# Decode delta rule begun with its inputs, its state loads on ACT's queue, all gate units first, and shorter pauses in both delta-rule chains

## The chip, the cores and the metric

The kernel runs on 1 core of one Trainium2 chip. The metric is the device time of one launch in microseconds (us). The times of the kernel before are the median of 3 runs; one execution was also taken with the hardware profiler, and all rows below are from it.

## What is computed

One step of a decoder layer over 256 prompt tokens and 8 decode tokens (264 columns, `TT`), width 2048. The input is normalised and projected by one wide matrix into everything the layer needs. Branch (A) is a sparse attention; branch (B) is a gated delta rule. The lines that matter here:

```
xn = rms_norm(x, norm_w);  q, kv, ..., z_a, qkv_b, a, b, z_b, gate_a, gate_b = split_proj(xn @ w_in)
# (B), prompt: chunks of tokens, per head
A  = strict_lower(kb k^T * L);  Tm = inverse(eye + A)
u  = Tm @ vb;  w = Tm @ (kb * exp(dec));  vn = u - w @ S
o  = (q * exp(dec)) @ S + lower(q k^T * L) @ vn
S  = S * exp(dl) + (k * exp(dl - dec))^T @ vn
# (B), decode: the same rule with one token, for 8 sequences, each with its own state S (8 heads of 128 x 128)
y_a = (o_A * silu(z_a)) @ w_pa;  y_b = (rms_norm(o_B) * silu(z_b)) @ w_pb
y   = x + (sigmoid(gate_a) * y_a + sigmoid(gate_b) * y_b) @ w_o
```

The outputs are y for prompt and decode tokens, the new caches, and the new delta-rule states of the prompt (`o_S`) and of the 8 decode sequences (`o_Ss`, stored two sequences at a time).

## The kernel before

**The weight stream.** All big projections run as a list of weight halves (`halves`, class `W`): 512 KB of f32 weights (8 contraction tiles of 128 x 128) are loaded by SP into `raw`, split into a rounded high part `hi` by ACT (line 332) and a rest `lo` by DVE (line 333), and multiplied by PE in 24 matmuls of 264 columns (three products for each tile) into an accumulator bank `acc`, of which there are two. The main loop at the end of the program writes, for each half, the load of four halves on, the split of two halves on, its first 12 matmuls, a `tick()`, its other 12 matmuls (with the evacuation after a unit's last half), and another `tick()`. So there are two ticks to a half.

**The order of units.** `ORDER` (line 30) lists the units of the second part of the program, a letter each: k a column block of the delta rule's q, k, v; g and G a block of gate a and gate b (`ev_gate`, tanh by ACT); z and Z a block of the output gate of branch A and of branch B (`ev_z`: tanh into a tile `zt` at line 1460, two multiplications, the second by oA or oB at line 1462, and a split into `oh` and `ol`); p and P a block of the products with w_pa and w_pb, which read oh and ol as their operand (`ev_y`). A k, g, G, z or Z unit has two halves, a p or P unit one. The evacuation of the first Z unit (line 1456) calls `tick()` until the prompt rule has marked oB: whatever of the two chains is not written by then is written there, with no weights between.

**The chains.** Everything else is written by generators. A tick advances each active one once; `yield n` means that it goes on n ticks later. Two chains start after the last k unit: `g_gdn_dec` (line 1342), the decode rule, first in each tick, and `g_gdn`, the prompt rule. The decode rule makes its vectors (L1346 to 1394), pauses, and then takes the states in four blocks of two sequences: a load `sst` of 1 MB (line 1401), 32 small matmuls `sw`, two copies `swr` by ACT (line 1411), transposes `swt`, the new value `dvn` (line 1418), four times transposes `vnb` and an update of the state by ACT (line 1432) and DVE (line 1433), and the store `o_Ss` from ACT's queue (line 1436). The prompt rule makes its decay rows and the products `kk` for 8 heads (into `At` and `aT`), sends the diagonal blocks of At through DRAM (`ad`) into `lanes`, solves them there in 31 steps of a product into `prod` (line 1203) and a sum (line 1204), sends the result through DRAM (`td`, lines 1210 and 1211) into `U` and into `TI`, a part of prod, completes the inverse (`inv`), forms `uw`, and goes over two chunks (`vn`, `dS`, `og`; the state `Sg` is another part of prod), stores `o_S` (line 1318), normalises, waits for the decode rule's `odec`, and writes oB (`ogt`, line 1337).

**What sets the order.** SP and POOL run their instructions in the order in which the program writes them (`manual_schedule`). PE, ACT and DVE are ordered by the framework, which takes of the instructions that are ready the one written first. Tiles come from a few tags with a fixed number of buffers: `slot()` (line 169) gives 8 KB tiles of tag s8, 13 buffers (xt, qkvr, ktk, vbt, qT, At, aT, lanes, prod, U, wT, oG, oB, sst, gate, oh, ol and others); tag "a" has 5 buffers (zt, swr, P1, kbe, yt and others); each PSUM tag has 2. A buffer goes back when the last reader of its tile is done, a store among them.

Of the kernel before, what the change touches and what calls it, by code (L numbers as in the profile page):

```python
# [26 lines left out]
BIG = 1e30  # L27
NCMP = 127
PAST = 2048
ORDER = "kgkkgkgkkkkkgkkkkkgkkkkkkkkkkGzzggzzgggGGgzzzGzggppppppGpppggppppppgpZZZGZGGZZZZGGGGPPGPGGGPPPPPPPPPPPPP"  # L30


class Cols:
# [111 lines left out]
def program(tc, A):  # L145
    nc = tc.nc
    V, S, T, G, SP = nc.vector, nc.scalar, nc.tensor, nc.gpsimd, nc.sync
# [42 lines left out]
    def C(name, parts=128):  # L190
        o, n = C0[name]
        return cst[0:parts, o:o + n]
# [7 lines left out]
    def tr(out, in_):  # L200
        n = in_.shape[0]
        T.transpose(out, in_, ident[0:n, 0:n])  # L202
# [925 lines left out]
    def g_gdn():  # L1128
# [23 lines left out]
        for h in range(9):  # L1152
            if h < 8:
                pr = PG("rrow")
                for t in range(2):
                    tr(pr[:, 128 * t:128 * t + 128], dec[:, t, h:h + 1].to_broadcast([128, 128]))
                er = tp.tile([128, 256], F32, name="er", tag="a", bufs=NA)
                S.activation(er, pr[:, 0:256], AF.Exp)
                l1 = tp.tile([128, 2, 128], F32, name="l1", tag="a", bufs=NA)
                l2 = tp.tile([128, 2, 128], F32, name="l2", tag="a", bufs=NA)  # L1160
                for t in range(2):
                    V.scalar_tensor_tensor(l1[:, t], pr[:, 128 * t:128 * t + 128], dec[:, t, h:h + 1], C("mlow"),
                                           ALU.subtract, ALU.add)
                    V.scalar_tensor_tensor(l2[:, t], pr[:, 128 * t:128 * t + 128], dec[:, t, h:h + 1], C("mup"),
                                           ALU.subtract, ALU.add)
                S.activation(l1, l1, AF.Exp, scale=-1.0)
                S.activation(l2, l2, AF.Exp)
                V.tensor_copy(edl[:, h, :], er.rearrange("p (c i) -> p c i", c=2)[:, :, 127])
                lm[h] = l1, l2, er
            yield  # L1170
            if h:
                h1 = h - 1
                l1, l2, er = lm.pop(h1)
                pk = PG("kk")
                for t in range(2):
                    sl = slice(128 * t, 128 * t + 128)
                    mm(pk[:, 128 * t:128 * t + 128], kTg[:, h1, sl], kTg[:, h1, sl])
                    mm(pk[:, 256 + 128 * t:384 + 128 * t], kTg[:, h1, sl], qTg[:, h1, sl])
                for t in range(2):
                    V.scalar_tensor_tensor(At[:, t, h1, :], pk[:, 128 * t:128 * t + 128], be[:, t, h1:h1 + 1], l1[:, t],  # L1180
                                           ALU.mult, ALU.mult)
                V.tensor_mul(aT[:, :, h1, :], pk[:, 256:512].rearrange("p (t i) -> p t i", t=2), l2)
                V.tensor_tensor(qTg[:, h1, 0:TP], qTg[:, h1, 0:TP], er, ALU.mult)
            yield 4
        del L["qkv", 1], kTg

        ad = dp.tile([4, 16, 32, 32], F32, name="ad")
# [32 lines left out]
        for t in range(2):  # L1220
            for hg in range(2):
                p1 = PG("inv")
                for hh in range(4):
                    h = 4 * hg + hh
                    rhs = U[:, t, h, :].rearrange("p (c k j) -> p c k j", c=2, k=2)[:, :, 1, :]
                    mm(p1[:, 64 * hh:64 * hh + 64].rearrange("p (c j) -> p c j", c=2), At[:, t, h, :], rhs)
                yield 6
                P1 = tp.tile([128, 256], F32, name="P1", tag="a", bufs=NA)
                S.activation(P1, p1[:, 0:256], AF.Copy)
                yield  # L1230
                p2 = PG("inv")
                for hh in range(4):
                    for c in range(2):
                        pr = slice(64 * c, 64 * c + 32)
                        o = 64 * hh + 32 * c
                        mm(p2[pr, o:o + 32], TI[pr, 8 * t + 4 * hg + hh, :], P1[pr, o:o + 32])
                p2v = p2[:, 0:256].rearrange("p (h c j) -> p h c j", h=4, c=2)
                for c in range(2):
                    V.tensor_scalar(U[64 * c:64 * c + 32, t, 4 * hg:4 * hg + 4, 64 * c + 32:64 * c + 64],
                                    p2v[64 * c:64 * c + 32, :, c, :], -1.0, None, ALU.mult)  # L1240
# [22 lines left out]
        for h in range(8):  # L1263
            kb = tp.tile([128, 2, 128], F32, name="kbe", tag="a", bufs=NA)
            for t in range(2):
                V.tensor_scalar(kb[:, t], ktk[:, t, h, :], bed[:, t, h:h + 1], None, ALU.mult)
            for t in range(2):
                V.tensor_scalar(ktk[:, t, h, :], ktk[:, t, h, :], kds[:, t, h:h + 1], None, ALU.mult)
            yield
            pu = PG("uw")  # L1270
            for t in range(2):
                mm(pu[:, 128 * t:128 * t + 128], U[:, t, h, :], vbt[:, t, h, :])
                mm(pu[:, 256 + 128 * t:384 + 128 * t], kb[:, t], U[:, t, h, :])
            yield 3
            V.tensor_copy(uu[:, :, h, :], pu[:, 0:256].rearrange("p (t d) -> p t d", t=2))
            S.activation(wT[:, h, :], pu[:, 256:512], AF.Copy)
        del L["vbt"]
# [3 lines left out]
        for t in range(2):  # L1281
            tok = slice(128 * t, 128 * t + 128)
            if t:
                for hg in range(2):
                    hs = slice(4 * hg, 4 * hg + 4)
                    pv = PG("vn")
                    for hh in range(4):
                        h = 4 * hg + hh
                        mm(pv[:, 128 * hh:128 * hh + 128], wT[:, h, tok], Sg[:, h, :])
                    V.tensor_sub(uu[:, t, hs], uu[:, t, hs], pv.rearrange("p (h d) -> p h d", h=4))  # L1290
                yield 4
            vn = uu[:, t]
            for hg in range(2):
                hs = slice(4 * hg, 4 * hg + 4)
                pS = PG("dS")
                for hh in range(4):
                    h = 4 * hg + hh
                    mm(pS[:, 128 * hh:128 * hh + 128], ktk[:, t, h, :], vn[:, h, :])
                yield 4
                po = PG("og")  # L1300
                for hh in range(4):
                    h = 4 * hg + hh
                    if t:
                        mm(po[:, 128 * hh:128 * hh + 128], qTg[:, h, tok], Sg[:, h, :], start=True, stop=False)
                    mm(po[:, 128 * hh:128 * hh + 128], aT[:, t, h, :], vn[:, h, :], start=t == 0, stop=True)
                yield
                if t == 0:
                    V.tensor_copy(Sg[:, hs, :], pS.rearrange("p (h d) -> p h d", h=4))
                else:
                    for hh in range(4):  # L1310
                        h = 4 * hg + hh
                        V.scalar_tensor_tensor(Sg[:, h, :], Sg[:, h, :], edl[:, h, t:t + 1],
                                               pS[:, 128 * hh:128 * hh + 128], ALU.mult, ALU.add)
                for hh in range(4):
                    h = 4 * hg + hh
                    S.activation(oG[:, t, h], po[:, 128 * hh:128 * hh + 128], AF.Copy, scale=qss[:, t, h:h + 1])
                yield 4
        G.dma_start(A["o_S"], Sg)
        so = tp.tile([128, 2, 8], F32, name="so", tag="so")
        ro = tp.tile([128, 2, 8], F32, name="ro", tag="ro")  # L1320
# [21 lines left out]
    def g_gdn_dec():  # L1342
# [52 lines left out]
        od = tp.tile([128, 64], F32, name="dod", tag="dod")  # L1395
        vn = tp.tile([128, 64], F32, name="dvn", tag="dvn")
        hb3 = lambda a: a.rearrange("p (h b) -> p h b", h=8)
        yield 88
        for b0 in range(0, NB, 2):
            ss = slot("sst", [128, 2, 8, 128])  # L1400
            G.dma_start(ss, A["stS"][b0 // 2])
            yield
            yield 7
            p3 = PGD("sw")
            for b in range(2):
                for h in range(8):
# [11 lines left out]
            V.tensor_sub(a3(vn), a3(u), pv[:, 0])  # L1418
            V.tensor_mul(a3(od), a3(vn), a3(kq))
            V.tensor_add(a3(od), a3(od), pv[:, 1])  # L1420
            yield 7
            for b in range(2):
                for hg in range(2):
                    p4 = PGD("vnb")
                    for hh in range(4):
                        c = (4 * hg + hh) * 8 + b0 + b
                        tr(p4[:, 128 * hh:128 * hh + 128], vn[:, c:c + 1].to_broadcast([128, 128]))
                    yield 3
                    for hh in range(4):
                        h = 4 * hg + hh  # L1430
                        c = h * 8 + b0 + b
                        S.activation(ss[:, b, h, :], ss[:, b, h, :], AF.Copy, scale=eb[:, 0, c:c + 1])  # L1432
                        V.scalar_tensor_tensor(ss[:, b, h, :], p4[:, 128 * hh:128 * hh + 128], k[:, c:c + 1],
                                               ss[:, b, h, :], ALU.mult, ALU.add)
                    yield 10
            S.dma_start(A["o_Ss"][b0 // 2], ss)
        so = tp.tile([128, 64], F32, name="dso", tag="qrd")
        S.activation(so, od, AF.Square)
# [127 lines left out]
    for w, kind in ((0, "kvs"), (1, "kvw")):  # L1566
        for j in range(4):
            proj(kind, j, ev_kv(w, j))
            if w == 0 and j == 0:
# [4 lines left out]
              P=iter(range(16)))  # L1574
    for i, c in enumerate(ORDER):
        j = next(at[c])
# [136 lines left out]
```

## Time and profile before

| | us |
|---|---|
| median of 3 runs | 1161.1 |
| lowest, highest | 1159.9, 1166.39 |
| the profiled execution | 1159.74 |
| its span | 1158.1 |

PE is the engine that works nearly all the time; the page also gives each engine's busy time in 40 equal slices of the span, so that a slice is 28.95 us. Each digit is the busy share in tenths. The rows that are read for the change are in a section of their own below.

### The profile page before, as it was taken

The numbers are of one execution on the slowest core, as the hardware profiler recorded it, in microseconds if no ns is written. First come the engines' busy times: TensorE is split into PE (matmuls) and PEld (weight loads), VectorE is DVE, ScalarE is ACT, GpSimd is POOL, SyncE is SP. The second block draws the span as 40 slices with busy tenths as digits, with TensorE's granted clock in tenths as the row PEclk, the third lists the DMA queues.
The fourth block names the chain that finished last, engine by engine and source line by source line (L and its number), as shares of the span: only waits on it lengthen the run. The fifth ranks groups of instructions, "written<-read, shape, count | busy, mean of one in ns | idle before, by whom it ended". The sixth has DMA issues, their size and how long they took to land.

```text
span 1158.1 us, 24872 instructions
## 1 busy us (share of the span) xinstructions
PE 1113.8 (96%) x9334; PEld 1064.9 (92%) x9334; DVE 725.6 (63%) x1538; ACT 571.4 (49%) x1126; POOL 142.0 (12%) x221
## 2 busy tenths in 40 slices
PE   4999999999999999999999999999996799999998
PEld 4989999999999897987889999998995699999998
DVE  3587665443667776863565676899475555567543
ACT  4455655445544765763455444433445544344332
POOL 4420344100001410122113000000100000000000
PEclk9999999999999999999999999999998899999999
DMA  8875576335446974578979345555653255556663
GB/s 300 261 221 157 191 218 204 102 128 166 157 134 191 236 192 131 164 225 206 343 297 364 127 159 164 195 165 185 193 183 127 94 183 184 180 182 220 201 238 127
DMA packets 76843, 222.86 MB, mean 192 GB/s; under 512 B 10465, under 2 KB 27370, under 8 KB 75186
## 3 DMA queue, kind: packets, MB, share of 16 engines
q1 hardware_dynamic: 59346, 164.36, 43.3%
q0 software_dynamic: 15360, 49.90, 14.9%
q10 hardware_dynamic: 2016, 7.01, 1.6%
q8 instruction: 73, 1.20, 0.4%
q14 instruction: 48, 0.39, 0.1%
HBM read 203.23 MB, written 17.99 MB: 191 GB/s over the span
## 4 chain that ended last, share of the span: by engine, by line
PE 76%; issue 11%; DVE 4%; DMA 4%; SPq 2%; ACT 1%; POOL 1%; POOLq 1%; ACTq 0%; DVEq 0%
PE acc L205 64%; DVE lanes L1204 1%; PE po L205 1%; PE pvo L205 1%; DVE lo L333 1%; PE gtr L202 1%; DMA raw<-w 1%; PE ps L205 1%; PE gsc L205 1%; DMA rawc<-ccmp 1%; SPq L385 1%; SPq L386 1%; POOLq L385 1%; DMA o_wk<-wk 1%; ACT sst L1432 1%
## 5 line engine op out<-in xcount | busy, mean ns | idle before, releaser
L332 ACT ACTIVATE hi<-raw 128x1024 fp32r<-128x1024 f32 (+1 forms) x250 | 264.3, 1057 | 352.3 <-PE acc L205 300.7
L205 PE MATMUL acc<-xh,hi 128*128 128x264 f32 (+1 forms) x1488 | 434.0, 292 | 1.0 <-ACT hi L332 1.0
L205 PE MATMUL acc<-xl,hi 128*128 128x264 f32 (+1 forms) x1488 | 427.3, 287 | 0.0
L205 PE MATMUL acc<-xh,lo 128*128 128x264 f32 (+1 forms) x1488 | 426.0, 286 | 0.1
L333 DVE TENSOR_TENSOR lo<-raw,hi 128x1024 fp32r<-128x1024 f32 (+1 forms) x250 | 304.4, 1218 | 192.5 <-ACT hi L332 190.6
L205 PEld LDWEIGHTS acc<-xh,hi 128*128 128x128 f32 (+1 forms) x1488 | 281.2, 189 | 9.6 <-issue 8.9
L205 PEld LDWEIGHTS acc<-xl,hi 128*128 128x128 f32 (+1 forms) x1488 | 281.5, 189 | 1.2 <-issue 0.6
L205 PEld LDWEIGHTS acc<-xh,lo 128*128 128x128 f32 (+1 forms) x1488 | 280.3, 188 | 2.3 <-issue 1.4
L205 PE MATMUL acc<-hi,w1h 128*128 128x254 f32 (+1 forms) x512 | 147.4, 288 | 14.9 <-ACT hi L409 14.9
L205 PE MATMUL acc<-lo,w1h 128*128 128x254 f32 (+1 forms) x512 | 146.2, 286 | 4.1 <-DVE lo L410 3.8
L205 PE MATMUL acc<-hi,w1l 128*128 128x254 f32 (+1 forms) x512 | 144.7, 283 | 0.0
L410 DVE TENSOR_TENSOR lo<-rawc,hi 128x512 fp32r<-128x512 f32 (+2 forms) x136 | 84.1, 658 | 51.0 <-ACT hi L409 42.7
L205 PEld LDWEIGHTS acc<-hi,w1h 128*128 128x128 f32 x512 | 97.5, 191 | 15.3 <-ACT hi L409 15.1
L409 ACT ACTIVATE hi<-rawc 128x512 fp32r<-128x512 f32 (+2 forms) x136 | 74.5, 599 | 58.5 <-PE acc L205 54.3
L205 PEld LDWEIGHTS acc<-lo,w1h 128*128 128x128 f32 x512 | 98.1, 192 | 5.6 <-DVE lo L410 5.4
L205 PEld LDWEIGHTS acc<-hi,w1l 128*128 128x128 f32 x512 | 98.0, 191 | 0.1
L386 POOL DMA_DIRECT2D rawc<-ccmp x125 | 67.4, 539 | 98.1 <-issue 71.4
L205 PE MATMUL acc<-oh,hi 128*128 128x264 f32 x256 | 72.7, 284 | 1.6 <-DVE gate L1482 1.6
L205 PE MATMUL acc<-ol,hi 128*128 128x264 f32 x256 | 72.8, 285 | 0.0
L205 PE MATMUL acc<-mh,hi 128*128 128x264 f32 x256 | 72.6, 284 | 0.0
L205 PE MATMUL acc<-ml,hi 128*128 128x264 f32 x256 | 72.5, 283 | 0.0
L205 PE MATMUL acc<-oh,lo 128*128 128x264 f32 x256 | 72.5, 283 | 0.0
(451 smaller groups left out, 1495.0 us busy)
## 6 DMA issues: line engine op xcount, KB each, us to landing
raw<-win SPq DMA_DIRECT2D x184, 512.0 KB, 3.4
raw<-wpab SPq DMA_DIRECT2D x32, 512.0 KB, 3.5
raw<-wo SPq DMA_DIRECT2D x32, 512.0 KB, 3.8
rawc<-ccmp SPq DMA_DIRECT2D x126, 128.0 KB, 3.1
rawc<-ccmp POOLq DMA_DIRECT2D x125, 128.0 KB, 3.2
raw<-w SPq DMA_DIRECT2D x8, 512.0 KB, 4.4
wk<-winK SPq DMA_DIRECT2D x8, 512.0 KB, 7.1
o_wk<-wk POOLq DMA_DIRECT2D x8, 512.0 KB, 8.7
```

The source lines that it names most:

```text
L202: T.transpose(out, in_, ident[0:n, 0:n])
L205: T.matmul(out, lhsT, rhs, start=start, stop=stop, **k)
L332: S.activation(self.hi, self.raw, AF.Copy)
L333: V.tensor_sub(self.lo, self.raw, self.hi)
L385: r = e.value_load(ptf[0:1, b * NPG + j:b * NPG + j + 1], min_val=0, max_val=159)
L386: e.dma_start(rawc[kv, b][j // 8][:, j % 8].rearrange("p s c g -> p (s c g)"), src[kv, bass.ds(r, 1)].rearrange("o d f -> (o d) f"))
L409: S.activation(h, src, AF.Copy)
L410: V.tensor_sub(l, src, h)
L1204: V.tensor_reduce(Lt[:, i, 0:i], pp.rearrange("p j c -> p c j"), AX.X, ALU.add, negate=True)
L1432: S.activation(ss[:, b, h, :], ss[:, b, h, :], AF.Copy, scale=eb[:, 0, c:c + 1])
```

## The change

Four things: the string of units has all G ahead of all P; the pauses of the prompt rule are shortened (4 to 2, 6 to 3, 3 to 2, and others, as shown); the decode rule no longer pauses 88 ticks before its first state load, and its pauses between steps go from 7, 7, 3 and 10 to 4 (with one tick less beside it), 2, 2 and 2; and the state loads are issued by ACT instead of POOL.

```diff
@@ -27,7 +27,7 @@
 BIG = 1e30
 NCMP = 127
 PAST = 2048
-ORDER = "kgkkgkgkkkkkgkkkkkgkkkkkkkkkkGzzggzzgggGGgzzzGzggppppppGpppggppppppgpZZZGZGGZZZZGGGGPPGPGGGPPPPPPPPPPPPP"
+ORDER = "kgkkgkgkkkkkgkkkkkgkkkkkkkkkkGzzggzzgggGGgzzzGzggppppppGpppggppppppgpZZZGZGGZZZZGGGGGGGGPPPPPPPPPPPPPPPP"
 
 
 class Cols:
@@ -1181,7 +1181,7 @@
                                            ALU.mult, ALU.mult)
                 V.tensor_mul(aT[:, :, h1, :], pk[:, 256:512].rearrange("p (t i) -> p t i", t=2), l2)
                 V.tensor_tensor(qTg[:, h1, 0:TP], qTg[:, h1, 0:TP], er, ALU.mult)
-            yield 4
+            yield 2
         del L["qkv", 1], kTg
 
         ad = dp.tile([4, 16, 32, 32], F32, name="ad")
@@ -1224,7 +1224,7 @@
                     h = 4 * hg + hh
                     rhs = U[:, t, h, :].rearrange("p (c k j) -> p c k j", c=2, k=2)[:, :, 1, :]
                     mm(p1[:, 64 * hh:64 * hh + 64].rearrange("p (c j) -> p c j", c=2), At[:, t, h, :], rhs)
-                yield 6
+                yield 3
                 P1 = tp.tile([128, 256], F32, name="P1", tag="a", bufs=NA)
                 S.activation(P1, p1[:, 0:256], AF.Copy)
                 yield
@@ -1271,7 +1271,7 @@
             for t in range(2):
                 mm(pu[:, 128 * t:128 * t + 128], U[:, t, h, :], vbt[:, t, h, :])
                 mm(pu[:, 256 + 128 * t:384 + 128 * t], kb[:, t], U[:, t, h, :])
-            yield 3
+            yield 2
             V.tensor_copy(uu[:, :, h, :], pu[:, 0:256].rearrange("p (t d) -> p t d", t=2))
             S.activation(wT[:, h, :], pu[:, 256:512], AF.Copy)
         del L["vbt"]
@@ -1288,7 +1288,7 @@
                         h = 4 * hg + hh
                         mm(pv[:, 128 * hh:128 * hh + 128], wT[:, h, tok], Sg[:, h, :])
                     V.tensor_sub(uu[:, t, hs], uu[:, t, hs], pv.rearrange("p (h d) -> p h d", h=4))
-                yield 4
+                yield 2
             vn = uu[:, t]
             for hg in range(2):
                 hs = slice(4 * hg, 4 * hg + 4)
@@ -1296,7 +1296,7 @@
                 for hh in range(4):
                     h = 4 * hg + hh
                     mm(pS[:, 128 * hh:128 * hh + 128], ktk[:, t, h, :], vn[:, h, :])
-                yield 4
+                yield 2
                 po = PG("og")
                 for hh in range(4):
                     h = 4 * hg + hh
@@ -1314,7 +1314,7 @@
                 for hh in range(4):
                     h = 4 * hg + hh
                     S.activation(oG[:, t, h], po[:, 128 * hh:128 * hh + 128], AF.Copy, scale=qss[:, t, h:h + 1])
-                yield 4
+                yield 2
         G.dma_start(A["o_S"], Sg)
         so = tp.tile([128, 2, 8], F32, name="so", tag="so")
         ro = tp.tile([128, 2, 8], F32, name="ro", tag="ro")
@@ -1395,12 +1395,11 @@
         od = tp.tile([128, 64], F32, name="dod", tag="dod")
         vn = tp.tile([128, 64], F32, name="dvn", tag="dvn")
         hb3 = lambda a: a.rearrange("p (h b) -> p h b", h=8)
-        yield 88
+        yield 2
         for b0 in range(0, NB, 2):
             ss = slot("sst", [128, 2, 8, 128])
-            G.dma_start(ss, A["stS"][b0 // 2])
-            yield
-            yield 7
+            S.dma_start(ss, A["stS"][b0 // 2])
+            yield 4
             p3 = PGD("sw")
             for b in range(2):
                 for h in range(8):
@@ -1418,21 +1417,21 @@
             V.tensor_sub(a3(vn), a3(u), pv[:, 0])
             V.tensor_mul(a3(od), a3(vn), a3(kq))
             V.tensor_add(a3(od), a3(od), pv[:, 1])
-            yield 7
+            yield 2
             for b in range(2):
                 for hg in range(2):
                     p4 = PGD("vnb")
                     for hh in range(4):
                         c = (4 * hg + hh) * 8 + b0 + b
                         tr(p4[:, 128 * hh:128 * hh + 128], vn[:, c:c + 1].to_broadcast([128, 128]))
-                    yield 3
+                    yield 2
                     for hh in range(4):
                         h = 4 * hg + hh
                         c = h * 8 + b0 + b
                         S.activation(ss[:, b, h, :], ss[:, b, h, :], AF.Copy, scale=eb[:, 0, c:c + 1])
                         V.scalar_tensor_tensor(ss[:, b, h, :], p4[:, 128 * hh:128 * hh + 128], k[:, c:c + 1],
                                                ss[:, b, h, :], ALU.mult, ALU.add)
-                    yield 10
+                    yield 2
             S.dma_start(A["o_Ss"][b0 // 2], ss)
         so = tp.tile([128, 64], F32, name="dso", tag="qrd")
         S.activation(so, od, AF.Square)
```

## Rows read from the trace of the kernel before

**Rows 1.** The page's busy shares of the engines and PE's slices.
```profile
PE 1113.8 (96%) x9334; PEld 1064.9 (92%) x9334; DVE 725.6 (63%) x1538; ACT 571.4 (49%) x1126; POOL 142.0 (12%) x221
...
PE   4999999999999999999999999999996799999998
```

**Rows 2.** Windows from 760 us on: busy us of each engine, clock, DMA.
```profile
core 0: us, PE busy (x) PEld busy (x) DVE busy (x) ACT busy (x) POOL busy (x), PEclk, DMA share, GB/s
760.00:815.00 55.00, 52.42 (x430) 51.93 (x429) 51.74 (x54) 19.98 (x23) 5.40 (x9) 1.00 0.60 186
861.95:914.40 52.45, 34.40 (x314) 30.18 (x313) 28.00 (x96) 32.81 (x117) 1.59 (x3) 0.87 0.28 107
914.40:1158.00 243.60, 240.28 (x1976) 240.07 (x1974) 136.44 (x191) 96.78 (x120) 0.00 (x0) 0.99 0.55 187
```

**Rows 3.** Same window, tile acc alone: PE, PEld, DVE, ACT.
```profile
861.95:914.40 52.45, 0.16 (x2) 0.03 (x1) 0.76 (x2) 0.65 (x2) 0.87 0.28 107
```

**Rows 4.** Waits, 760 to 980: who waited for whom; us, times, longest.
```profile
POOL o_S L1318 <- DVE prod L1312: 44.0, 1, 44.0
```

**Rows 5.** Timeline of PE: start, us, instruction, [idle before and its releaser].
```profile
759.05 0.28 PE L205 MATMUL acc<-xh,lo 128*128 128x264 f32 x1
759.17 0.28 PE L205 MATMUL acc<-oh,lo 128*128 128x264 f32 x1
...
864.00 0.39 PE L205 MATMUL uw<-vbt,U 128*128 128x128 f32 x2
864.23 0.39 PE L205 MATMUL uw<-U,kbe 128*128 128x128 f32 x2
...
865.44 1.08 PE L205 MATMUL sw<-sst,wq 128*32 128x128 f32 x32
...
894.41 1.94 PE L205 MATMUL sw<-sst,wq 128*32 128x128 f32 x32 [7.50 <-DMA sst<-stS]
...
914.81 0.42 PE L205 MATMUL acc<-xl,hi 128*128 128x264 f32 x1
915.03 0.42 PE L205 MATMUL acc<-xh,lo 128*128 128x264 f32 x1
```

**Rows 6.** Timeline of ACT in the gap.
```profile
895.09 4.49 ACT L1432 ACTIVATE sst<-sst,deb 128x128 f32<-128x128 f32 x15 [5.41 <-PE sw L205]
...
909.89 0.63 ACT L1411 ACTIVATE swr<-sw 128x256 f32<-128x256 f32 x2
...
912.46 0.65 ACT L1460 ACTIVATE zt<-acc 128x264 f32<-128x264 f32 x2
```

**Rows 7.** Timeline of DVE: first lane step, z7's and the first Z's product.
```profile
729.56 0.15 DVE L1203 TENSOR_TENSOR prod<-lanes 64x1 f32<-64x1 f32 x1 [2.22 <-DMA lanes<-ad]
...
750.89 0.42 DVE L1462 SCALAR_TENSOR_TENSOR zt<-zt,qT 128x264 f32<-128x264 f32 x1
...
927.96 1.12 DVE L1462 SCALAR_TENSOR_TENSOR zt<-zt,oB 128x264 f32<-128x264 f32 x3
```

**Rows 8.** DMA issues: queue, count, KB each, median us from issue to landing.
```profile
raw<-win SPq DMA_DIRECT2D x184, 512.0 KB, 3.4
...
sst<-stS POOLq DMA_DIRECT2D x4, 1024.0 KB, 7.4
o_Ss<-sst ACTq DMA_DIRECT2D x4, 1024.0 KB, 4.2
```

**Rows 9.** Tile sst: issue of its stores in ns; landing of all its DMAs.
```profile
L1436 ACTq DMA_DIRECT2D o_Ss<-sst x4: 338/346/363, 854.1 to 920.5; - x4
...
DMA to landing us min/median/max: 4.1/5.8/9.2
```

**Rows 10.** Windows of the lane solve, tile prod alone: PE, PEld, DVE, POOL.
```profile
729.50:756.98 27.48, 0.00 (x0) 0.00 (x0) 11.24 (x36) 0.00 (x0) 1.00 0.51 165
756.98:803.70 46.72, 0.00 (x0) 0.00 (x0) 29.23 (x26) 0.00 (x0) 1.00 0.54 176
```

**Rows 11.** Timeline of POOL: the td stores and the first load of U.
```profile
803.87 0.53 POOL L1210 DMA_DIRECT2D td<-lanes  x1 [77.49 <-DVE lanes L1204]
...
810.67 0.68 POOL L1215 DMA_DIRECT2D U<-td  x1 [4.10 <-DMA td<-lanes]
```

## The prediction

> **What bounds the kernel now.** I read the shares and the slices first: TensorE (PE) is busy 96% of the span, nothing else is above 63%, and apart from the first slice only the 31st and 32nd of 40 (868 to 926 us) show it well short of full [rows 1]. So the kernel is bound by PE, and a change can win only what PE is idle or slow. The windows say where that is: from 861.95 to 914.40 PE is busy 34.40 of 52.45 us at a granted clock of 0.87, while the stretch after it, to the end, is busy 240.28 of 243.60, and 760 to 815 is busy 52.42 of 55.00 [rows 2]. In the 52.45 us gap there are two weight matmuls in all [rows 3]: PE does the two delta rules' own work and nothing else, although 240 us of weight matmuls are still to come.
>
> Why are they not taken? The waits of 760 to 980 and the timelines answer. The last decode block's states are loaded behind the store of the prompt state in POOL's queue, which itself waits 44.0 us [rows 4]; PE sits 7.5 us until that load lands, at 894.41 [rows 5]. The first gate unit that reads oB has its sums ready long before, and ACT is free (5.41 us of idle before 895.09), yet its tanh into zt runs at 912.46, directly after the last swr at 909.89 [rows 6]. zt and swr share the five buffers of tag "a". That order says: buffers of a tag go out in the order in which the program is written, so a tile written late cannot overtake one written early, even where a buffer is free. zt was written after the last swr and waited for it. The same rule will govern the changed kernel, with the 13 buffers of tag "s8" in the main part.
>
> **The unit of reckoning.** A tick is half a weight half: 12 matmuls at 0.12 us (759.05 to 759.17 [rows 5]), 1.45 us of PE. I count the steps from the tick at which the decode delta rule starts, and add up the pauses of the two chains as written. Kernel before to after: last kk 49 to 33; first sst load 97 to 11; second load 166 to 35, its store 235 to 59; third load 235 to 59; first step of the lane solve 59 to 41; U and td 83 to 65; last store of states 374 to 107; oB about 382 to 163. The first oB reader is written at step 129, and drains what is not done: 253 ticks without weights before, 34 after. By steps alone the gap of 52.45 us is gone.
>
> **What that gives back.** In the gap PE has 312 matmuls that must be done somewhere: 96 of sw, three groups of 1.08 us, and 216 others. At full clock these stand 0.112 us apart (two in 0.22 us from 864.23) [rows 5], so 24.2 + 3.2 = 27.4 us is work and 52.45 - 27.4 = 25.0 us comes back. The weights after the gap start slow (0.22 us apart at 914.81 against 0.12 [rows 5], for some 15 matmuls), another 1.5 us. Of 760 to 815 the 55.00 - 52.42 = 2.6 us idle are not counted twice if that stretch becomes idle for another reason. Together 29.1 us.
>
> **What it brings in.** Count the s8 buffers at step 59, where the third sst load is written. Taken are: qT (which holds oA), the q part of qkv, ktk, vbt, two tiles of gate a, one of gate b, At, aT, oh, ol: 11. The k part of qkv went free after the last kk and the first sst after its store; the second sst block and lanes take these two, 13. So prod (step 41, after the second sst) gets a buffer only when the second sst block has been stored, and the third sst (step 59) only when something else goes. prod stays to the end of the prompt rule (it holds TI and Sg). lanes goes when the lane solve is over and both td stores have landed. qT goes after the last unit that reads oA, z7; but z7's zt is written at step 68, after the third block's swr at step 63, and by the order in [rows 6] waits for that swr, which waits for the third load. So qT cannot help, and the third load waits for the whole lane solve. Until then z7 keeps one of the two accumulator banks, its column of oh and ol is missing, and p0, the first reader of oh [rows 5], stops at its last eighth; all later units stand behind p0's bank. PE runs dry.
>
> When does it? p0 starts at 759.17 before [rows 5]. Work of two sst blocks moves ahead of it: per block 32 sw matmuls in 1.08 and 20 transposes (swt, vnb) at 0.112, 2.2 [rows 5], so 3.3 us, 6.6 for two. Two units on one accumulator bank cost about 2 (an estimate: each waits for the evacuation before it, a tanh of 0.33 [rows 6] and some time to be noticed on both sides), and p0 runs 21 matmuls, 2.5 us. PE stops at 759 + 6.6 + 2 + 2.5 = 770.
>
> When does it go on? The lane solve starts at step 59, 729.56, before [rows 7], 2.2 us of it a wait. After, it waits for the second sst block's store, written at the same step 59: 727.3 + 6.6 of moved work + 4.2 to land [rows 8], with 3 for the chain's own waits, 741. It took 27.48 us to 756.98 and then 46.72 in which its multiplications and sums alone held DVE 29.23 [rows 10]; with no weights on PE there are no lo splits between, so 28 + 29.2 + 1.5 = 58.7, end 800. The td stores need 6.5 (803.87 to the 810.67 at which U's load waits no more [rows 11]): 806.5. Load of the third block, 4.1 to 9.2 to land [rows 9]: 812.5 at the middle; sw, swr, zt, oh some 3.5: 816. Idle 46, plus the 2 above, plus 1.5 of slow clock after so long a stop, less 1.0 as one sw runs in it: 48.5 us.
>
> **Sum.** 1159.7 (the profiled execution; its span is 1158.1 and 1.6 lies around it; the median 1161.1 is 1.4 above) + 48.5 - 29.1 = 1179.1.
>
> **The other parts.** The order of units (the two P among the last G, all G now first) costs nothing: both kinds have equal matmuls, and the stretch is full of PE [rows 2]; bounds -1.6 to +1.6 us from the 3.3 us idle in it. The shorter pauses add no instruction. The loads cost ACT an issue each, 0.346 as its stores show [rows 9]: 4 x 0.35 = 1.4 us, hidden, since ACT is busy 19.98 of the 55 us of 760 to 815 [rows 2]; without that cover 1.4 us. Worse is a load that waits for a buffer on ACT, with hi splits queued behind it: two split halves, 5.8 us, are ahead, and PE stands anyway for want of oh; 0 to 5.8, taken 0.
>
> The transfer itself: 1024 KB take 7.4 us from POOL's queue, 512 KB 3.4 from SP's [rows 8], one rate. The Trainium skill ("DMA: Bandwidth & Descriptors", section "Issuing engines are not separate DMA queues") says that a DMA runs on the same 16 engines whoever issues it, so that another issuer saves only the time of issuing. By that alone the move would leave the 7.5 us wait and the sum would be 1186.6; but the 44.0 us wait in POOL's queue ahead of the load shows that a queue's order can cost more than its issues, and my sum takes the wait as gone.
>
> **Rivals.** (1) The other side: the buffers do not bind. If z7's zt can be had ahead of the third swr, qT's buffer is free at about 754 (z7's product with oA is at 750.89 [rows 7]), the third load starts while units run, and PE never dries. Then 1159.7 - 26.5 + 1.4 for the issues = 1135. For it: a load of 7.4 us has 16 steps of cover; against it: the 5.41 us in which ACT was free and zt was not begun [rows 6]. It decides at the point where z7's evacuation comes before the lane solve's end.
> (2) Stall and return cancel. The lane solve starts as early as before (729.5, 11.5 us earlier, prod finding a buffer without the second store) and the td stores land in 2.2 us (4.3 less): 1179.1 - 15.8 = 1163. For it: the store may land early; against: the count of 13.
> (3) The gap stays too: the prompt chain, started late behind the stall, ends as late against the weights as before, and the stall is added whole: 1159.7 + 48.5 - 1.5 = 1207. Against it: after 816 PE still has at least the 240.28 us that stood behind the gap [rows 2], and the chain from the td stores to the first use of oB took 803.87 to 927.96, 124 us, stalls and all [rows 7, 11].
>
> **How the numbers follow.** Forecast 0.70, at 1179. Its own bounds: start of the solve 4 us either way (landing 4.1 to 9.2), td 3 to 7, third load 4 to 9, start of the stall 3 either way: stall 34 to 60, so 1164 to 1192. Rival (1) 0.16, (2) 0.10, (3) 0.04. Leaving out (1) and (3) would leave out 0.20 before the forecast's own tails, so the range goes down to 1134 and up to 1192. A run can tell 0.5% from no change, 5.8 us: (1) is faster, (2) and the lowest end of the forecast the same, the rest slower: 0.16, 0.12, 0.72.
>
> **What would show it.** Right: a stretch of 35 to 60 us from about 770 without acc matmuls; in it DVE busy with the lane solve alone; the third sst load's issue right behind the landing of td; z7's zt directly after the third swr; no gap at the first oB reader; PE as full as now after it. Wrong: the third load issued before the solve ends, or z7's zt before its swr (then (1)); a solve that starts before the second store has landed (then (2)); a second stretch without weights after 860 (then (3)).

## The result

The changed kernel takes 1176.93 us (median of 4 runs, 1175.76 to 1177.57) against 1161.69 for the kernel before, in four runs beside it: a ratio of 1.0124 with a 95% interval of 1.0092 to 1.0155, 15 us slower. Its profiled execution took 1175.76 us, with a span of 1174.1.

The page of the changed kernel: the shares, PE's busy tenths in 40 slices, and PE's granted clock in the same slices.

```profile
PE 1109.9 (95%) x9334; PEld 1062.7 (91%) x9334; DVE 726.7 (62%) x1538; ACT 571.0 (49%) x1126; POOL 140.2 (12%) x217
...
PE   4999999999999999999999999933999999999998
...
PEclk9999999999999999999998999975999999999999
```

Against [rows 1] the dent has moved: it was in the 31st and 32nd slice, it is now in the 27th and 28th (763 to 822 us), it is deeper, and the slices in which the first Z units run are full. The windows say the same; first all engines (PE, PEld, DVE, ACT, POOL, clock, DMA), then the tile acc alone.

```profile
core 0: us, PE busy (x) PEld busy (x) DVE busy (x) ACT busy (x) POOL busy (x), PEclk, DMA share, GB/s
776.34:815.54 39.20, 2.94 (x37) 2.10 (x37) 23.85 (x22) 5.59 (x19) 1.42 (x2) 0.55 0.17 53
820.00:1172.00 352.00, 350.90 (x3015) 348.07 (x3013) 204.59 (x338) 152.98 (x245) 3.29 (x6) 1.00 0.53 180
```

```profile
776.34:815.54 39.20, 0.00 (x1) 0.00 (x1) 0.43 (x1) 0.38 (x1) 0.55 0.17 53
```

For 39.2 us no weight matmul runs; PE works 2.9 us (the third block's sw and swt), DVE 23.9. From 820 on PE is idle 1.1 us in 352. The sum closes: from 600 us to 1.6 us before the end PE was idle 23.6 us before (window 556.50, busy 532.95) and is idle 42.2 now (572.50, busy 530.28). That is 18.7 us more idle and 2.7 us less busy time, which I put down to the slow clock of the old gap (0.87 [rows 2]) being gone: 16.0, the difference of the spans.

The timelines of the stretch: PE, ACT, DVE and POOL of the changed kernel (start, us, instruction, idle time before it and what ended it).

```profile
776.06 0.28 PE L205 MATMUL acc<-oh,lo 128*128 128x264 f32 x1
809.06 1.93 PE L205 MATMUL sw<-sst,wq 128*32 128x128 f32 x32 [32.71 <-DMA sst<-stS]
814.54 1.11 PE L202 MATMUL swt<-cst,swr 128*128 128x128 f32 x4 [3.55 <-ACT swr L1410]
815.54 0.59 PE L205 MATMUL acc<-oh,hi 128*128 128x264 f32 x1
```

```profile
739.97 0.35 ACTq L1435 DMA_DIRECT2D o_Ss<-sst  x1
...
804.30 0.33 ACTq L1401 DMA_DIRECT2D sst<-stS  x1
809.73 4.49 ACT L1431 ACTIVATE sst<-sst,deb 128x128 f32<-128x128 f32 x15 [36.23 <-PE sw L205]
814.12 0.63 ACT L1410 ACTIVATE swr<-sw 128x256 f32<-128x256 f32 x2
814.65 0.38 ACT L1459 ACTIVATE zt<-acc 128x264 f32<-128x264 f32 x1
```

```profile
744.68 0.14 DVE L1203 TENSOR_TENSOR prod<-lanes 64x1 f32<-64x1 f32 x1
...
799.37 1.02 DVE L1209 COPY lanes<-lanes 64x1024 f32<-64x1024 f32 x1
```

```profile
799.62 0.87 POOL L1210 DMA_DIRECT2D td<-lanes  x1 [85.14 <-DVE lanes L1204]
...
818.80 0.68 POOL L1215 DMA_DIRECT2D U<-td  x1 [17.57 <-DVE dod L1419]
```

One reads it from the end. PE's next weight matmul (815.54) reads oh, whose last column is made from z7's zt (814.65); zt comes directly after the third block's swr (814.12); swr needs sw (809.06), which waited 32.71 us for the load; the load was issued at 804.30, when the td stores of the lane solve had landed; the solve ran from 744.68 to 799.4, and began 4.7 us after the second block's store was issued (739.97; such a store takes 4.2 to land [rows 8]). U is zeroed only at 816.45, right after z7's product has read qT for the last time (815.96; in the kernel before 752.09 after 751.31), so the prompt chain waited for z7 too, 12 us behind the landing of td. (The changed kernel is one line shorter, so L1401 is still the load but L1410 is swr and L1459 zt.)

### The profile page after: what moved, and what is told of

Its sections match the earlier page's. It is cut to its first block, busy times and chain, and to the rows that moved or that the text cites. A ratio compares the mean times of both kernels' runs of the same rounds, so it can differ in the third digit from the quotient of the medians.

```text
span 1174.1 us, 24864 instructions
## 1 busy us (share of the span) xinstructions
PE 1109.9 (95%) x9334; PEld 1062.7 (91%) x9334; DVE 726.7 (62%) x1538; ACT 571.0 (49%) x1126; POOL 140.2 (12%) x217
```

## The experiments

Each kernel was timed beside the kernel before; the ratio is the kernel's to it. The kernel before had medians of 1159.9 to 1163.3 in these groups of runs, so times of different groups compare to some 3 us.

| kernel | median us | ratio (95% interval) |
|---|---|---|
| the changed kernel | 1176.93 | 1.0124 (1.0092 to 1.0155) |
| pause of 12 ahead of the third block | 1149.16 | 0.9896 (0.9873 to 0.9918) |
| solve cut to 7 of 31 steps | 1138.03 | 0.9810 (0.9784 to 0.9836) |
| decode part alone | 1153.51 | 0.9940 (0.9918 to 0.9962) |
| prompt pauses alone | 1170.24 | 1.0081 (1.0058 to 1.0103) |
| pause of 32 ahead of the second block | 1148.23 | 0.9887 (0.9857 to 0.9917) |
| prompt pauses and loads on ACT | 1160.00 | 0.9987 (0.9969 to 1.0005) |
| order of units alone | 1160.81 | 0.9998 (0.9980 to 1.0016) |
| loads on ACT alone | 1155.57 | 0.9944 (0.9928 to 0.9961) |
| changed kernel, loads on SP | 1184.02 | 1.0183 (1.0143 to 1.0223) |
| changed kernel, swr out of tag a | 1148.90 | 0.9877 (0.9836 to 0.9918) |
| pause of 32, later loads on POOL | 1141.72 | 0.9815 (0.9777 to 0.9854) |

### Is the stall from the order of buffers?

**A pause of 12 ticks ahead of the third block** (e1) writes the third load behind z7's evacuation and behind U.

```diff
         for b0 in range(0, NB, 2):
+            if b0 == 4:
+                yield 12
             ss = slot("sst", [128, 2, 8, 128])
```

> The changed kernel with one pause of 12 ticks more before the third state block, so that its load and its swr are written after z7's evacuation and after U; nothing else. Theory (the third load waits for the lane solve, and z7's zt for the third swr): z7 is evacuated at about 760, p0 does not stop, the 39.2 us without weight matmuls from 776.34 to 815.54 are gone, the third load follows the landing of td at about 806 and nobody waits for it. If the prompt chain ends in time for the first Z: 1177 - 39 = 1138 us. Rival of the same theory's second half: the prompt chain (oB written at 950 to 955 in the changed kernel) does not come earlier when the weights do, and the idle time turns up again ahead of the first Z, 912 to 945: 1160 to 1175. Rival (the stall is not from this order): a stall of 30 to 40 us stays at 776 and the time stays at 1177.

Measured: 1149.16, 28 us under the changed kernel, between the theory's 1138 and the rival's 1160. The stall is gone: the same window, and the one ahead of the first Z.

```profile
776.34:815.54 39.20, 36.78 (x303) 36.39 (x302) 39.06 (x41) 13.48 (x15) 0.00 (x0) 1.00 0.49 160
879.20:893.00 13.80, 10.50 (x84) 9.19 (x83) 13.47 (x54) 4.09 (x10) 0.00 (x0) 1.00 0.27 101
```

z7's zt runs at 758.27. But 39 us do not come back, only 28. The solve started at 743.00 as in the changed kernel, and now shares DVE with the weights' splits:

```profile
743.00:817.05 74.05, 0.00 (x0) 0.00 (x0) 40.55 (x62) 0.00 (x0) 1.00 0.53 173
```

That is the solve's own tile (prod): 40.6 us of DVE work drawn out over 74 us, as in the kernel before (729.56 to 803.58), against 39.9 in 54.8 in the changed kernel, where PE's stop left DVE to it. So the prompt chain ends 15 us earlier (last copy into oB at 939.9 against 954.8) where the weights come 39 earlier, and 13.7 us without weight matmuls open ahead of the first Z (879.29 to 892.97); another 8.3 (826.91 to 835.25) lie at the third load, where sw stands on PE ahead of weight matmuls:

```profile
833.39 1.94 PE L205 MATMUL sw<-sst,wq 128*32 128x128 f32 x32 [6.48 <-DMA sst<-stS]
```

The rival of the second half was right in kind, though smaller than it forecast.

**swr out of tag a** (e10) leaves the loads on ACT and their places in the program as they are, and takes away what z7's zt waits for (two of a block's four copies are written two ticks later, its first transpose two earlier).

```diff
-            rows = [tp.tile([128, 256], F32, name="swr", tag="a", bufs=NA) for _ in range(2)]
-            for b in range(2):
-                S.activation(rows[b], p3[:, 256 * b:256 * b + 256], AF.Copy)
-            yield 2
             p5 = PGD("swt")
             for i in range(4):
-                tr(p5[:, 128 * i:128 * i + 128], rows[i // 2][:, 128 * (i % 2):128 * (i % 2) + 128])
+                row = tp.tile([128, 128], F32, name="swr", tag="dsq", bufs=2)
+                S.activation(row, p3[:, 128 * i:128 * i + 128], AF.Copy)
+                if i == 1:
+                    yield 2
+                tr(p5[:, 128 * i:128 * i + 128], row)
```

> The changed kernel with swr in four tiles of 128 columns in the two buffers of tag dsq instead of two tiles of 256 columns in tag a (four ACT copies for two in each block, some 0.6 us of ACT more in each); nothing else, the loads on ACT and their places in the program stay. Theory (z7's zt waits for the third swr's buffer): zt no longer waits, runs at about 762, qT goes free at about 765, the third load is issued there instead of at 804, the stall of 39 us is gone; the lane solve still starts at about 744, so a gap of about 15 us stays ahead of the first Z as with the 12-tick pause: 1150 us (1143 to 1158). Rival (ACT's queue or p0's bank alone): the stall stays, 1172 to 1180.

Measured: 1148.90. ACT's timeline:

```profile
759.85 0.37 ACT L1459 ACTIVATE zt<-acc 128x264 f32<-128x264 f32 x1
...
762.70 0.34 ACTq L1401 DMA_DIRECT2D sst<-stS  x1
```

zt comes 55 us earlier, the third load follows it by 3 us (qT's buffer), and 28 us of the time go with the stall. Little else was changed, so the stall hung on tag a. It was the order in which its five buffers are given out and not their number: in the changed kernel, between z6's last split (753.17) and the third swr (814.12), the only tile of the tag that is still to be read is dcv (until 870.7). Without the stall, 8.1 us without weights are left at the fourth load (834.13 to 842.25) and 8.6 ahead of the first Z (883.37 to 891.99).

**Loads on SP** (e9) was meant to tell the same from ACT's queue, and does not.

```diff
-            S.dma_start(ss, A["stS"][b0 // 2])
+            SP.dma_start(ss, A["stS"][b0 // 2])
```

> The changed kernel with the four state loads issued by SP instead of ACT; nothing else. In the changed kernel the third load waits on ACT until 804.30 and z7's zt stands behind it and behind the third swr, so two causes fit: the order in which buffers of tag a are given out, or ACT's queue standing at the load. Theory (the order of the a buffers): ACT is free, zt still comes directly after the third swr, the stall of about 39 us at 776 stays, and the time is 1172 to 1185, the upper part if SP's weight loads behind the waiting load come late. Rival (ACT's queue): z7's zt runs at about 755 to 762, the third load takes qT's buffer at about 765, no stall, 1140 to 1155.

Measured: 1184.02, in the theory's interval, but for another reason than the one it was meant to show. SP stood at the third load from 741.6 to 795.42 with all weight loads behind it:

```profile
741.22 0.33 SPq L327 DMA_DIRECT2D raw<-win  x1
795.42 0.33 SPq L1401 DMA_DIRECT2D sst<-stS  x1
```

```profile
800.32 1.94 PE L205 MATMUL sw<-sst,wq 128*32 128x128 f32 x32 [44.02 <-DMA sst<-stS]
```

so PE ran out of weights at 756.30, before z7's sums were complete, stood 44.0 us, and had its next weight matmul at 804.43. What it shows is the price of a load that waits in a queue with weight loads behind it: some 7 us more than on ACT.

### What ends the stall?

**The solve cut to its first 7 steps** (e2; the other 24 products and sums are left out, so the inverse is not the reference's).

```diff
         for i in range(1, 32):
+            if i < 8:
-            pp = prod[0:64, 0:i * i].rearrange("p (j c) -> p j c", c=i)
-            V.tensor_tensor(pp, Lt[:, 0:i, 0:i], La[:, i, 0:i, None].to_broadcast([64, i, i]), ALU.mult)
-            V.tensor_reduce(Lt[:, i, 0:i], pp.rearrange("p j c -> p c j"), AX.X, ALU.add, negate=True)
+                pp = prod[0:64, 0:i * i].rearrange("p (j c) -> p j c", c=i)
+                V.tensor_tensor(pp, Lt[:, 0:i, 0:i], La[:, i, 0:i, None].to_broadcast([64, i, i]), ALU.mult)
+                V.tensor_reduce(Lt[:, i, 0:i], pp.rearrange("p j c -> p c j"), AX.X, ALU.add, negate=True)
```

> The changed kernel with the lane solve cut to its first 7 of 31 steps; the other 24 products and sums are left out, the pauses between them are kept, so the order of everything else is as in the changed kernel. The inverse, and with it the prompt part of the delta rule, is not computed fully. Theory (the third load waits for the end of the solve and the td stores): the solve, 744.7 to 799.6, shrinks to about 3 us, td lands at about 755, the third load is issued there, and the stall of 39.2 us shrinks to 0 to 5; the prompt chain is some 45 us earlier as well, so no other gap can open: 1177 - 37 = 1140 us (1136 to 1146). Rival (the stall comes from the decode chain's own length or from ACT's queue): the stall stays over 20 us and the time over 1155.

Measured: 1138.03, and ACT's timeline has the same sequence as the changed kernel, 48 us earlier:

```profile
755.66 0.33 ACTq L1402 DMA_DIRECT2D sst<-stS  x1
...
766.37 0.63 ACT L1411 ACTIVATE swr<-sw 128x256 f32<-128x256 f32 x2
766.89 0.38 ACT L1460 ACTIVATE zt<-acc 128x264 f32<-128x264 f32 x1
```

zt still stands right behind swr, but nothing waits long for either; no stretch over 5.3 us is without weight matmuls after 600 us. The end of the solve ends the stall.

### Which part of the change does it?

**The decode part alone** (e3: begun with its inputs, loads on ACT, its shorter pauses; the prompt pauses and the order of units stay).

```diff
-        yield 88
+        yield 2
         for b0 in range(0, NB, 2):
             ss = slot("sst", [128, 2, 8, 128])
-            G.dma_start(ss, A["stS"][b0 // 2])
-            yield
-            yield 7
+            S.dma_start(ss, A["stS"][b0 // 2])
+            yield 4
...
-            yield 7
+            yield 2
...
-                    yield 3
+                    yield 2
...
-                    yield 10
+                    yield 2
```

> The kernel before with the decode part of the change alone (begun with its inputs, loads on ACT, its shorter pauses); the order of units and the prompt rule's pauses are those of before. Theory: the buffers are taken in the same order (k part of qkv and the first block's buffer go to the second block and lanes, prod waits for the second block's store, the third load for the lane solve), so the stall of 35 to 45 us at 770 to 820 is there; the prompt chain is written later than in the changed kernel, so the time is 1177 to 1190. Rival (the prompt rule's shorter pauses make the stall): no stall, under 1150.

Measured: 1153.51, faster than before, and both expectations missed it. ACT and DVE:

```profile
734.80 0.35 ACTq L1435 DMA_DIRECT2D o_Ss<-sst  x1
...
739.80 0.34 ACTq L1401 DMA_DIRECT2D sst<-stS  x1
```

```profile
762.89 0.14 DVE L1203 TENSOR_TENSOR prod<-lanes 64x1 f32<-64x1 f32 x1
```

With the longer prompt pauses prod is first written at step 59, the step at which the third load is written, and in one tick the decode chain comes first. So the third load takes the second block's buffer (739.80, right behind its store), z7 is not held, and it is prod that waits, for qT's buffer, until z7 is done. No stall at 776; instead the solve ends late (846.3), and a gap of 35.3 us opens ahead of the first Z (859.42 to 894.66). One step's difference in the order of two requests decides which of the two chains pays.

**The prompt pauses alone** (e4).

```diff
-            yield 4
+            yield 2
         del L["qkv", 1], kTg
...
-                yield 6
+                yield 3
                 P1 = tp.tile([128, 256], F32, name="P1", tag="a", bufs=NA)
...
```

> The kernel before with the prompt rule's shorter pauses alone; order of units and decode rule are those of before. Theory: no state block is loaded before the lane solve, so prod finds a buffer, the solve starts some 18 steps, about 23 us, earlier (about 706), and there is no stall at 776. The gap ahead of the first Z is ended by the last state block, whose load stands behind the o_S store in POOL's queue; that store comes some 20 us earlier, so the gap of 52.4 us shrinks to about 32: 1161 - 20 = 1141 us (1135 to 1150). Rival (the decode chain's own 374 steps set the gap, not the queue): 1161 within 3 us.

Measured: 1170.24, slower by 0.8%, where I had forecast 20 us of gain; the rival's 1161 missed too. The solve does start earlier (716.7 against 729.56 [rows 7]). POOL shows what went wrong:

```profile
887.37 0.56 POOL L1318 DMA_DIRECT2D o_S<-prod  x1 [84.26 <-DVE prod L1312]
887.93 1.68 POOL L1401 DMA_DIRECT2D sst<-stS  x3
```

The o_S store is now written ahead of three state loads instead of two, and it runs no earlier than before (887.4 in both), so three blocks come after it, and the gap ahead of the first Z ends at 923.22 instead of 914.45. Why a solve that starts 13 us earlier does not bring that store forward, no run shows.

**The same with the loads on ACT** (e6), and **the loads on ACT alone** (e8):

```diff
-            G.dma_start(ss, A["stS"][b0 // 2])
+            S.dma_start(ss, A["stS"][b0 // 2])
```

> The kernel before with the prompt rule's shorter pauses and with the state loads issued by ACT; nothing else. With the shorter pauses alone it took 1170, three of the four loads then standing behind the o_S store on POOL (issued at 887.9 to 889.1). Theory (POOL's written order holds the loads back): on ACT they go when a buffer is free, some 20 to 40 us earlier, oB comes at about 915 and the gap of 41.7 us ahead of the first Z halves: 1150 us (1142 to 1158). Rival (the decode chain's buffers or its written place hold them, not the queue): 1166 to 1172.

> The kernel before with the state loads issued by ACT alone. Theory (as in the prediction: the last two loads stand behind the o_S store in POOL's queue, 887.9 and 888.5): they go some 15 to 25 us earlier, PE's wait of 7.5 us for the load is gone, the gap of 52.4 us shrinks to about 37: 1146 us (1140 to 1154). Rival (only the issue moves, the blocks are held by their buffers): within 2 us of 1160.

Measured: 1160.00 and 1155.57; off POOL's queue the loads are worth 10 us where three stood behind o_S, and 6 where two did, half or less of what I forecast, and in both runs outside the theory's range and the rival's. In e6 they go at 873 to 882 instead of 888 to 889, and the gap of 41.7 us is 26.7. In e8 the last two go at

```profile
885.85 0.37 ACT L1316 ACTIVATE oG<-og,qss 128x128 f32<-128x128 f32 x1 [1.92 <-PE og L205]
885.86 0.34 ACTq L1401 DMA_DIRECT2D sst<-stS  x1
886.42 0.33 ACTq L1401 DMA_DIRECT2D sst<-stS  x1
```

only 2 us before the 887.9 and 888.5 of the kernel before. Off POOL's queue they stand in ACT's: each goes right behind a copy of the prompt rule (oG), the first of which waited 1.92 us for PE, and in e6 the same pair stands the same way (873.21 and 873.22). Whether their buffers came free much earlier no run shows. PE's wait of 7.5 us for such a load is 0.7 here and the gap ahead of the first Z 43.0 us instead of 52.3, but 6.5 us without weights open at the first load (817.20 to 823.66), where sw waits on PE.

**The order of units alone** (e7) is the one line `ORDER` of the diff.

> The kernel before with the new order of units alone (all G ahead of all P). The stretch in which the order differs is full of PE work on both sides, so 1160 within 2 us; a rival that P between G hides something would show 3 us or more either way.

Measured: 1160.81, a ratio of 0.9998. It costs and brings nothing.

So alone the decode part is worth -0.6%, the prompt pauses +0.8%, the order 0.0%; together they are +1.2%, and by another mechanism than any of them alone.

### What keeps both gains?

**A pause of 32 ticks ahead of the second block** (e5): only the first block comes before the solve.

```diff
         for b0 in range(0, NB, 2):
+            if b0 == 2:
+                yield 32
             ss = slot("sst", [128, 2, 8, 128])
```

> The changed kernel with a pause of 32 ticks more ahead of the second state block (instead of 12 ahead of the third): only the first block comes before the lane solve, the second is written at step 67, after U (65), its swr at 71, after z7's zt (68). Theory (the order in which s8 and a buffers are asked for sets both the stall and the start of the solve): prod takes the first block's buffer, the solve starts at about 717 instead of 743 to 745, z7 takes its zt at about 755, there is no stall at 776, the other three blocks run from about 795 to 880, oB is written by 905 to 915, and little or no gap is left ahead of the first Z: 1137 us (1132 to 1145), below the 1149 of the 12-tick pause. Rival (the blocks, now late, hold the five buffers of tag a ahead of kbe, and the prompt chain waits for them): oB at 930 or later, 1148 to 1160.

Measured: 1148.23, above the expected 1132 to 1145 and at the lower edge of the rival's range, with the last of oB written at 929.0 (the profiled execution, 1144.34, was the fastest of four). The solve starts at 715.78, there is no stall at 776, and from 811 us on no stretch without weight matmuls is longer than 4.4 us. One long wait is left, 7.2 us without weights at 803.6, at the second load on ACT and at its sw on PE:

```profile
799.73 0.34 ACTq L1403 DMA_DIRECT2D sst<-stS  x1
800.20 1.06 ACT L332 ACTIVATE hi<-raw 128x1024 fp32r<-128x1024 f32 x1 [3.43 <-DMA td<-lanes]
```

```profile
809.01 1.94 PE L205 MATMUL sw<-sst,wq 128*32 128x128 f32 x32 [5.38 <-DMA sst<-stS]
```

ACT stands at the load until td has landed, with a split behind it, and sw stands on PE ahead of weights that are ready.

**The later loads on POOL** (e11), behind td and U and ahead of o_S, with more room ahead of sw.

```diff
+            if b0 == 2:
+                yield 32
             ss = slot("sst", [128, 2, 8, 128])
-            S.dma_start(ss, A["stS"][b0 // 2])
-            yield 4
+            (G if b0 else S).dma_start(ss, A["stS"][b0 // 2])
+            yield 8 if b0 else 4
```

> The changed kernel with the pause of 32 ticks ahead of the second block, the loads of the last three blocks on POOL (behind the td stores and U's loads, ahead of the o_S store), and 8 ticks instead of 4 from such a load to its sw. With the pause alone it took 1148 (span 1142.7); there PE stood 5.4 us at 803.6 to 809.0 for the second load, and ACT 3.4 us at the load while hi splits waited behind it. Theory (a load that waits on ACT holds up the splits, and sw stands ahead of ready weights on PE): the two waits shrink to 1 or 2 us, the solve starts at 716 as before: span 1137 to 1141, median 5 us below the 1148. Rival (the wait is for td's landing whoever issues): 1146 to 1150.

Measured: 1141.72 (1141.18 to 1142.12), a ratio of 0.9815: faster than both kernels, 35 us under the changed one. The wait at this place is still 3.9 us, now of another instruction:

```profile
812.65 1.15 PE L205 MATMUL inv<-U,At 128*128 128x64 f32 x8 [3.92 <-DMA U<-td]
```

so the split's wait went, and PE still waits for what td brings through DRAM, now at inv. The run changes the queue and the ticks ahead of sw together and does not tell which of the two helped. The median came down by 6.5 us, the span of the profiled execution by 2.2.

## Why the prediction was right

Forecast 1179, measured 1176.93; against the profiled execution before, +19.4 forecast and +16.0 measured. The range, 1134 to 1192, takes in a gain as well as a loss; what bears the prediction out is the place of the stall and the chain behind it.

- **The order of buffers** was read from one place, zt directly behind swr though ACT was free [rows 6]. It carried the prediction, and e10 shows it by itself.
- **The count of 13** held: prod waited for the second block (first step at 744.68, forecast 741), the third load for the td stores. That the same count comes out otherwise when two requests fall on one step, I did not see; e3 showed it.
- **Where PE stops**: 776.3, forecast 770. p0 began at 773.55. The 759.17 that I read as p0's start [rows 5] is its third matmul. The moved work of two blocks is as counted (104 matmuls). What I missed is 36 weight matmuls that run ahead of p0's first one here and ran after it before (p0 had begun at 756.27, between others), 4.3 us of useful work, and 1.6 us of small waits at the first block (685.67 and 693.29). The two waits on one accumulator bank were 1.30 us each, forecast 2 together.
- **Where it goes on**: 815.5, forecast 816. Solve's end 799.4 (800), td 804.2 (806.5), load landed 809.0 (812.5), then sw, swr, zt and p0 6.5 instead of 3.5, as ACT did 15 state updates (4.49 us) ahead of swr. Two errors of 3 us cancelled here, so that the end came out to half a microsecond by luck.
- **What comes back**: no long gap is left ahead of the first Z, and the old one, with its slow clock, is gone; the 25.0 + 1.5 of the sum. By an estimate from the trace the stall cost some 43 us (39.2 without weights, 2.6 at the two banks, 1.6 at the first block, 1.0 of slow start, less 1.5 of sw and swt in it) and some 27 came back, against 48.5 and 29.1.
- **The mis-sized term** is the stall: 39.2 us without weights instead of 46, for the start of it. Its slow start after the stop is as forecast: weight matmuls 0.22 us apart until 817.7 (the lower of PE's two levels, 1.2 GHz), then 0.12 (2.4 GHz), as after the old gap [rows 5]; the granted clock over the stop was 0.55.
- **The order of units** at nothing: 0.9998 (e7).
- **The loads on ACT**, taken at nothing: in the changed kernel their wait lies inside the stall. In e1, e5 and e10, where the stall is gone, 8.3, 7.2 and 8.1 us without weights lie at a load. My bound of 5.8 was for splits behind the load, and those waited 5.22, 3.43 and 3.82 us on ACT; what it left out is sw, which stands on PE ahead of the weights until the load has landed (6.48, 5.38 and 6.25 us). My reading that the 44.0 us wait in POOL's queue [rows 4] held the last loads was half wrong: off that queue they went only 2 us earlier (e8). The transfer takes 7.0 us (the median of four) from ACT's queue against 7.4 from POOL's [rows 8]. That agrees with the Trainium skill ("DMA: Bandwidth & Descriptors", section "Issuing engines are not separate DMA queues"), by which the issuer changes only the time of issuing. The order in the issuer's queue is another matter: moving the loads was worth 6 us in e8 and 7 the other way in e9.
- **Rival (1)** was the right mechanism for the way out, and mispriced: without the stall the kernel takes 1149, not 1135 (e1, e10). Its price left out that a solve which starts at 744 and shares DVE with the splits ends at 817 to 824, that oB is then late for the first Z (13.7 and 8.6 us without weights), a small form of rival (3), and that a load still costs 8 us.
- **Slips of the working**, none of which moves the forecast by more than about 1 us: the bounds as listed give a stall of 36 to 59 us and a time of 1167 to 1190, not 34 to 60 and 1164 to 1192; the 4.1 of [rows 9] is a store's landing (the four loads took 5.1 to 9.2); 803.87 to 810.67 [rows 11] is 6.8 us, not 6.5.

## What to carry to other kernels

Where tiles of a tag are handed out in the order of the program, a step that is written earlier takes a buffer from one that used to come first: count the buffers at each request on both chains, and look for a circle in which A waits for B's buffer and B stands behind A in another tag. An earlier start of a side chain is a gain only if what it pushes back (here the solve, a store in POOL's queue, a gate's evacuation) is not what the main stream waits for next. Shorter pauses add no work but change who is first; try them one chain at a time, as their effects do not add.

## What was unexpected

Two edits of -0.6% and +0.8% made +1.2% together. A queue that stands costs by what is behind it: weight loads on SP (44.0 us of PE), splits on ACT (3.43 us in e5), and three state loads behind a store on POOL (10 us, e4 against e6). And the lane solve's 40 us of DVE work take 54.8 us when PE stops and 74 when it does not, so that a stall of PE pays part of itself back.
